# A two-layer diffusion backbone on one core: output projections with a PSUM bank per half, layer 1's last rows, another pool order in the context FFN

## The chip, the core and the metric

The kernel runs on one core of a Trainium2 chip. Its engines work side by side and wait for each other through semaphores: TensorE (PE; PEld is its weight load) multiplies matrices into PSUM, VectorE (DVE), ScalarE (ACT) and GpSimd (POOL) work on elements, and SyncE (SP) issues most DMAs. POOL issues DMAs too. The time of a kernel is the device time of one execution in microseconds (us); the median of several runs counts. A profile is the record of one execution.

## What is computed

Two layers over 1024 latent rows of 1024 numbers (`x`) and 256 context rows (`ctx`). The reference, cut to the flow:

```python
for l in range(DEPTH):                                  # DEPTH = 2
    ctx_out = l < DEPTH - 1                             # the context only in layer 0
    h_lat = modulate(x_lat, m_lat[0], m_lat[1])
    ...
    y_lat, y_ctx = even_mixer(...) or odd_mixer(...)    # attention, then @ w_out
    x_lat = layer_norm(DN_ALPHA * x_lat + m_lat[2] * y_lat, ln_g[l, 0], ln_b[l, 0])
    f_lat = conv_ffn(modulate(x_lat, m_lat[3], m_lat[4]), ffn_w_up[l], ...)
    x_lat = layer_norm(DN_ALPHA * x_lat + m_lat[5] * f_lat, ...)
    if ctx_out:
        ...                                             # the same for x_ctx
return x_lat

def conv_ffn(h, w_up, conv_w, conv_b, w_down):          # 3 taps along the rows
    u = h @ w_up                                        # 1024 -> 2 * 2816
    ...
    a, g = jnp.split(acc, 2, axis=-1)
    return (jax.nn.silu(g) * a) @ w_down
```

All is float32. The kernel keeps that precision with three matmuls for each product: an operand is split into a high part (`h`: a cast on ACT) and a low part (`l`: the rest, a subtraction on DVE or POOL), and `mm3` adds high by high, high by low and low by high. "A weight split" below is one such cast and one such subtraction of 128x512 numbers.

## The kernel before

The stages follow one another: layer 0's projections and attention, its output projection (`l0_out`), the context FFN (`ffn`), the latent FFN of layer 0, then layer 1's projection, attention, output projection (`l1_out`) and FFN. The change touches both output projections and the starts of the two FFNs behind them.

**`out_project`** is the output projection of both layers. It goes over tiles of 128 rows: in layer 0 the two context tiles 8 and 9, then the latent tiles 0 to 7; in layer 1 the latent tiles 0 to 7. For each tile SP loads the old row `x` and the attention's output `yr` in two halves; ACT and POOL split it into `yh` and `yl`. TensorE makes 48 matmuls of 128x512 into the tile `o`: 8 blocks `k` of the contraction by 2 halves `h` of the columns by 3. They run with `k` outside, except in the last tile, where `h` is outside. Behind the last matmul DVE evicts both halves: `hst` (times the gate), a `scalar_tensor_tensor` with the old row, `bn_stats`. `ln` normalises: `mv` on DVE, `rs` on POOL, then the row on DVE (in the last tile half on DVE, half on ACT, with `nm`). `finish` of a tile comes behind the matmuls of the next one: eight transposes (`tr`) on TensorE, eight steps on ACT that modulate them into `hst`, the parts `h2l..` or `h3l..` that the FFN multiplies, sums and differences of blocks (`tt`, called T below) that POOL stores in DRAM, and the store of the row `x`. In the last tile `finish` of the tile before is called between the halves. The hooks are `mid` (in the third tile), `after` (behind the last tile's matmuls) and `last` (at the end).

**End of layer 0.** `after` is `first_up`: it loads and splits the up weights of the first three steps of the context FFN (f = 0, 1, 2; two loads and eight splits each) and makes `u` of two steps (`ctx_up`). `ffn` then goes over 22 steps f: load a down row (`row(f)`, a tile `raw`) and the up weights two steps ahead (`raws[f + 2]`), make `u[f]`, run the convolution of step f - 1 on ACT (`centre`: `a` and `g`) and DVE (`sides`), Silu on ACT, multiply into `gT`, split weights, and multiply step f - 2 down into `d`. The stage's order on each engine is that of the code. Its first DMA is the gate. Where its buffers lie in SBUF follows from the order in which its pools are opened: `acc` (gate, rows), `fraw` (raw weights), `fc` (`a`, `g`), `fg` (`gT`). They take the room that the projection's pools leave, and the first use of a buffer waits for the last use of what lay there.

**End of layer 1.** The FFN behind it multiplies blocks of rows (0 to 511 and 512 to 1023) in seven products for each step, into the PSUM tiles `x`, `y`, `q` and `v`, from `h3lah/h3lal`, `h3lbh/h3lbl` and four operands T0 to T3. `build_B1` makes a tile's share of T0 to T3 for the latent tiles 4 to 7, the last one's straight into the ring of weights, the others' in `tt` (one buffer), stored to `T1` in DRAM and loaded back (`gk`, `go`, `ua`, `ug`) when all are there; ACT and DVE then split them (`T0h`, `T0l`). In `l1_out`, `mid` is `weights` (the up weights of two steps in parts `E[p]`), `after` is `first_x` (the first part of `x` for p = 0 and 1) and `last` is `rest` (more splits). The FFN opens with matmuls that start `y` and `q` (`adds`: dummies of the right shape), a copy of `x` into `y` on ACT, and the second part of `x`, from `h3lbh`; then `v` from T0, `y` from T1, `q` from T2 and T3.

## Time and profile before

| | us |
|---|---|
| median of 3 runs (2916.8 to 2927.06) | 2923.64 |
| the profiled execution | 2927.96 |
| its span | 2926.1 |
| busy: TensorE, DVE, ACT, POOL | 2765.7, 2117.6, 1383.0, 691.5 |
| mean granted clock of TensorE | 0.976 |

The profile's times count from the start of the span, in us. A row of the timeline has its start, its duration, the engine, the line, the operation with what it writes and reads, and in brackets how long the engine had been idle and what ended that. SP's and POOL's DMA rows give the time of the issue, not of the transfer. Matmuls overlap, so their pace is the distance of their starts. In layer 0 the output projection runs from about 754 to 875, in layer 1 from about 2153 to 2250.

### The profile page before, as it was taken

The numbers are of one execution on the slowest core, as the hardware profiler recorded it, in microseconds if no ns is written. First come the engines' busy times: TensorE is split into PE (matmuls) and PEld (weight loads), VectorE is DVE, ScalarE is ACT, GpSimd is POOL, SyncE is SP. The second block draws the span as 40 slices with busy tenths as digits, with TensorE's granted clock in tenths as the row PEclk, the third lists the DMA queues.
The fourth block names the chain that finished last, engine by engine and source line by source line (L and its number), as shares of the span: only waits on it lengthen the run. The fifth ranks groups of instructions, "written<-read, shape, count | busy, mean of one in ns | idle before, by whom it ended". The sixth has DMA issues, their size and how long they took to land.

```text
span 2926.1 us, 45178 instructions
## 1 busy us (share of the span) xinstructions
PE 2765.7 (95%) x16596; PEld 2254.8 (77%) x16596; DVE 2117.6 (72%) x3832; ACT 1383.0 (47%) x2597; POOL 691.5 (24%) x967
## 2 busy tenths in 40 slices
PE   6989999899999999999999987989998899999997
PEld 4877777777788988888888876866677688887886
DVE  4876366667588778888877656557766788888778
ACT  3221255567435655555553342257753545555541
POOL 2611143354451000000001013435544011111002
PEclk8999999999999999999999998989999999999999
DMA  8468711032567653333367526732244455555862
GB/s 261 141 188 275 229 39 41 11 128 94 160 161 241 207 169 107 119 107 114 117 236 272 163 83 195 226 106 64 65 132 146 126 172 164 176 171 201 325 219 93
DMA packets 370502, 456.87 MB, mean 156 GB/s; under 512 B 26137, under 2 KB 265017, under 8 KB 368745
## 3 DMA queue, kind: packets, MB, share of 16 engines
q1 hardware_dynamic: 342808, 369.40, 40.7%
q0 software_dynamic: 24576, 82.89, 8.2%
q8 instruction: 130, 2.13, 0.3%
q10 hardware_dynamic: 2896, 1.70, 0.2%
q14 instruction: 92, 0.75, 0.1%
HBM read 337.98 MB, written 115.93 MB: 155 GB/s over the span
## 4 chain that ended last, share of the span: by engine, by line
PE 68%; issue 10%; DVE 9%; DMA 6%; ACT 5%; POOL 1%; SPq 0%; ACTq 0%; DVEq 0%; POOLq 0%
PE q L1691 8%; PE x L1691 8%; PE y L1691 7%; PE S L762 4%; PE v L1691 4%; PE pv L907 3%; PE T L893 3%; PE dy L2354 3%; PE mm L401 2%; PE d L402 2%; PE d L403 2%; PE d L401 2%; PE mm L402 2%; PE mm L403 2%; PE dx L2354 2%
## 5 line engine op out<-in xcount | busy, mean ns | idle before, releaser
L786 POOL TENSOR_SCALAR P<-P,rin 128x640 f32<-128x640 f32 (+3 forms) x288 | 250.2, 873 | 347.3 <-DVE rin L785 324.0
L1665 DVE TENSOR_TENSOR w<-raw,w 128x512 fp32r<-128x512 f32 x308 | 207.3, 687 | 84.2 <-ACT w L1663 84.1
L112 ACT CAST w<-raw 128x512 fp32r<-128x512 f32 x315 | 183.3, 620 | 171.3 <-PE d L403 60.9
L113 DVE TENSOR_TENSOR w<-raw,w 128x512 fp32r<-128x512 f32 x299 | 194.2, 690 | 70.3 <-ACT w L112 68.2
L762 PE MATMUL S<-k,q 64*128 64x256 f32 (+2 forms) x1824 | 192.4, 338 | 16.9 <-DVE nm L2643 8.1
L783 ACT ACTIVATE P<-P,nm 128x641 f32<-128x641 f32 (+4 forms) x208 | 161.3, 777 | 83.0 <-DVE nm L2643 47.8
L1663 ACT CAST w<-raw 128x512 fp32r<-128x512 f32 x308 | 182.2, 621 | 13.8 <-DVE raw L1670 7.4
L762 PEld LDWEIGHTS S<-k,q 64*128 64x128 f32 x1824 | 136.1, 189 | 52.6 <-issue 17.8
L773 ACT COPY PT<-T 128x512 f32<-128x512 f32 (+1 forms) x250 | 134.0, 565 | 78.9 <-PE T L893 76.7
L907 PE MATMUL pv<-PT,v 128*64 128x128 f32 x2016 | 134.1, 281 | 16.3 <-ACT PT L773 14.1
L893 PE MATMUL T<-ident,P 128*128 128x128 f32 x1008 | 137.2, 283 | 7.9 <-POOL P L786 3.4
L907 PEld LDWEIGHTS pv<-PT,v 128*64 128x64 f32 x2016 | 109.5, 138 | 42.4 <-ACT PT L773 23.0
L401 PE MATMUL d<-w,w 128*128 128x512 f32 x352 | 138.0, 392 | 0.0
L403 PE MATMUL d<-w,w 128*128 128x512 f32 x352 | 137.7, 391 | 0.0
L402 PE MATMUL d<-w,w 128*128 128x512 f32 x352 | 137.6, 391 | 0.0
L785 DVE RECIPROCAL rin<-den 128x1 f32<-128x1 f32 x288 | 46.2, 162 | 121.0 <-ACT P L783 118.1
L893 PEld LDWEIGHTS T<-ident,P 128*128 128x128 f32 x1008 | 111.0, 143 | 28.5 <-issue 14.6
L771 DVE COPY PT<-T 128x512 f32<-128x512 f32 (+1 forms) x166 | 110.4, 666 | 30.7 <-PE T L893 20.6
L1691 PE MATMUL q<-T2h,w 128*128 128x512 f32 x352 | 117.7, 396 | 5.5 <-ACT q L1906 3.9
L1691 PE MATMUL q<-T3h,w 128*128 128x512 f32 x352 | 118.3, 397 | 4.0 <-DVE ug L2309 3.9
L2354 PE MATMUL dy<-w,w 128*128 128x512 f32 x528 | 120.8, 390 | 0.6 <-DVE w L113 0.6
L2643 DVE CUSTOM_DVE_ANT_0 P<-S,msk,snk 128x640 f32<-128x640 f32 (+1 forms) x128 | 103.7, 846 | 16.9 <-PE S L762 13.5
(417 smaller groups left out, 7802.2 us busy)
## 6 DMA issues: line engine op xcount, KB each, us to landing
raw<-in_up_dram SPq DMA_DIRECT2D x132, 512.0 KB
raw<-in_down_dram SPq DMA_DIRECT2D x59, 512.0 KB
raw<-g SPq DMA_DIRECT2D x44, 512.0 KB
raw<-G SPq DMA_DIRECT2D x38, 512.0 KB
araw<-in_ada_w_dram SPq DMA_DIRECT2D x32, 512.0 KB
raw<-in_w_in_dram SPq DMA_DIRECT2D x28, 512.0 KB
g<-cv POOLq DMA_DIRECT2D x22, 512.0 KB, 3.0
G<-go POOLq DMA_DIRECT2D x44, 256.0 KB, 2.7
```

The source lines that it names most:

```text
L112: nc.scalar.copy(hi, s)
L113: (lo_eng or nc.vector).tensor_sub(lo, s, f32(hi))
L401: nc.tensor.matmul(ps, lh, rh, start=first, stop=False)
L402: nc.tensor.matmul(ps, lh, rl, start=False, stop=False)
L403: nc.tensor.matmul(ps, ll, rh, start=False, stop=last)
L762: self.nc.tensor.matmul(outs[a], q[r, x, qs], k[r, y, ks], start=(i == 0), stop=(i == 2))
L786: nc.gpsimd.tensor_scalar(P[:, :n], P[:, :n], rin, 1.0, ALU.mult, ALU.mult)
L893: nc.tensor.transpose(ps[:, s * 128 : (s + 1) * 128], P[a][:, cols[i + x] : cols[i + x] + 128], self.ident,)
L907: nc.tensor.matmul(O[a * HD : (a + 1) * HD], v_of(a, vts[i + x]), pT[:, s * 128 : (s + 1) * 128], start=(i + x == 0), stop=(i + x == m - 1 ...
L1665: nc.vector.tensor_sub(half(i, 1), src[i], f32(half(i, 0)))
L1691: nc.tensor.matmul(ps, w[:, a, s], r[b][:, k], start=first and k + i == 0, stop=k == 3 and i == 2, skip_group_check=True,)
L2354: nc.tensor.matmul(banks[q][t], ga[i][:, a, c], wd[i][:, b], start=q < 2 and f + k == 0, stop=f == HF - 1 and k == 2, skip_group_check=True,)
```

## The change

1. Each half of `o` is a PSUM tile of its own (`o0`, `o1`). In all tiles but the first the half is the outer loop, and the eviction of a half stands behind its own last matmul. In layer 1 these tiles have one buffer each instead of two of the double size; the bank that this leaves holds `y` in the pool of `x`.
2. `first_up` ends with a Silu of one column.
3. `ffn` opens its pools in the order `fc`, `fg`, `fraw`, `acc`.
4. In layer 1, tile 6's T is made in buffers of `yh` and `yl` instead of `tt` and stored in two DMAs. `weights` splits one more part of `E[1]`; `first_x` starts `y` and copies `x` into it; `rest` makes the second part of `x`; the FFN's opening keeps only the dummies of `q`.

```diff
@@ out_project
-            ps = self.t(pp, [128, 2, 512], "o")
+            ps = [self.t(pp, [128, 512], f"o{h}") for h in range(2)]
...
-            if t == order[-1]:
+            if t != order[0]:
                 kh.sort(key=lambda x: x[1])
...
+            g = gate_of(t)
+            s6 = self.t(st, [128, 2, 6], "s6", bufs=3)
             for i, (k, h) in enumerate(kh):
...
                 self.mm3(
-                    ps[:, h], yh[:, k], yl[:, k], ws[k, h][:, 0], ws[k, h][:, 1],
+                    ps[h], yh[:, k], yl[:, k], ws[k, h][:, 0], ws[k, h][:, 1],
                     k == 0, k == KT - 1,
                 )
...
+                if k == KT - 1:
+                    s = slice(h * 512, (h + 1) * 512)
+                    tt = self.t(st, [128, 512], "hst", bufs=3)
+                    nc.vector.tensor_mul(tt, ps[h], g[:, s])
+                    nc.vector.scalar_tensor_tensor(
+                        x[:, s], x[:, s], ALPHA, tt, ALU.mult, ALU.add
+                    )
+                    nc.vector.bn_stats(s6[:, h, :], x[:, s])
@@ first_up
+                warm = self.t(st, [128, 1], "warm")
+                nc.scalar.activation(warm, self.mhalf[:, :1], AF.Silu)
@@ ffn
-            ap = es.enter_context(self.pool("acc"))
-            raw = es.enter_context(self.pool("fraw", bufs=4))
             cvp = es.enter_context(self.pool("fc", bufs=2))
             gp = es.enter_context(self.pool("fg", bufs=3))
+            raw = es.enter_context(self.pool("fraw", bufs=4))
+            ap = es.enter_context(self.pool("acc"))
@@ build_B1
+        elif t == NLAT - 2:
+            m = [
+                self.t(st, [128, KT, 128], x, bufs=2).rearrange("p (m k) j -> p m k j", m=2)
+                for x in ("yh", "yl")
+            ]
+            tt = [m[i // 2][:, i % 2] for i in range(4)]
...
-        if t < NLAT - 1:
+        if t == NLAT - 2:
+            for i in range(2):
+                nc.gpsimd.dma_start(
+                    dT[2 * i : 2 * i + 2, :, t - 4].rearrange("m p k j -> p m k j"), m[i]
+                )
+        elif t < NLAT - 2:
             nc.gpsimd.dma_start(dT[:, :, t - 4].rearrange("m p k j -> p m k j"), m)
@@ layer 1's FFN, opening
                     for p in pre if m == 1 else []:
-                        X, Y, Q = YQ[p] = (early["x", p],) + tuple(
-                            self.t(pu, [128, 512], f"{x}{p}") for x in "yq"
-                        )
-                        adds(Y, Q)
-                        nc.scalar.copy(Y, X)
-                        self.product(early[p][0][2], b21, X, False)
+                        Q = self.t(pu, [128, 512], f"q{p}")
+                        YQ[p] = early["x", p], early["y", p], Q
+                        adds(Q)
@@ l1_out
-            pp = es.enter_context(self.pool("op1", bufs=2, space=PSUM))
+            pp = es.enter_context(self.pool("op1", bufs=1, space=PSUM))
...
-                for p, i in ((0, 0), (1, 0), (0, 2), (0, 1)):
+                for p, i in ((0, 0), (1, 0), (0, 2), (1, 2), (0, 1)):
                     self.some_parts(E[p][1], [i])
 
             def first_x():
                 for p in range(2):
-                    E["x", p] = self.t(px, [128, 512], f"x{p}")
-                    self.product(E[p][0][0], h2l[:2], E["x", p], True)
+                    X, Y = (self.t(px, [128, 512], f"{x}{p}") for x in "xy")
+                    E["x", p], E["y", p] = X, Y
+                    ah = h2l[0]
+                    nc.tensor.matmul(Y, ah[:, 0, :128], ah[:, 0], start=True, stop=True)
+                    self.product(E[p][0][0], h2l[:2], X, True)
+                    nc.scalar.copy(Y, X)
 
             def rest():
+                for p in range(2):
+                    self.product(E[p][0][2], [v[:, :, 0] for v in h2l[2:]], E["x", p], False)
                 self.some_parts(E[0][1], [4, 3, 5, 6])
-                self.some_parts(E[1][1], [2])
```

What this moves on the engines, at three places. First SP at the end of layer 0, with what each DMA waits for: the last up load of `first_up`, then the context FFN's gate, its first down row and the up weights of step 3. Before:

```order
L1644 DMA raw_10012<-in_up_dram 128x8x128 [waits DVE_49]
L159 DMA gate_10182<-ada_89 128x1024 [waits PE_49]
L1440 DMA raw_10188<-in_down_dram 128x1024 [waits DMAHW2_49,PE_49]
L1644 DMA raw_10190<-in_up_dram 128x8x128 [waits DVE_49]
L1644 DMA raw_10192<-in_up_dram 128x8x128 [waits DMAHW4_49,DVE_49]
```

Now:

```order
L1657 DMA raw_10022<-in_up_dram 128x8x128 [waits DVE_49]
L159 DMA gate_10194<-ada_89 128x1024 [waits DMASW7_49,DVE_49,DMAHW7_49,PE_49,Activation_49]
L1442 DMA raw_10200<-in_down_dram 128x1024 [waits DMAHW2_49]
L1657 DMA raw_10202<-in_up_dram 128x8x128
L1657 DMA raw_10204<-in_up_dram 128x8x128 [waits DMAHW4_49]
```

The order is the same. The gate waited for TensorE alone and now waits for a DMA of POOL's queue (the store of tile 7's row), DVE, SP's own load of that row, TensorE and ACT, since the gate's buffer lies where that row lay; the loads behind it lost most waits of their own.

ACT at the same place, from the half row of tile 7 (`x`) on: `hst` are tile 7's transposes, `a` and `g` step 0 of the context FFN, `w` its down weights. Before:

```order
L372 ACTIVATE x_9869<-x_9869,nm_9943,rs_9940 128x512
L1556 ACTIVATE hst_10130<-tr_10125,m1ab_572_3199 128x128 x4
L1556 ACTIVATE hst_10143<-tr_10138,m1ab_572_3199 128x128 x4
L1444 ACTIVATE a_10196<-u_10026,cc_369_1685,cc_367_1681 128x256
L1444 ACTIVATE g_10198<-u_10026,cc_369_1685,cc_367_1681 128x256
L1488 ACT_TABLE_LOAD
L1488 ACTIVATE g_10198<-g_10198 128x256
L1495 CAST gT_10206<-a_10196 128x256
L112 CAST w_10209<-raw_10188 128x512
```

Now:

```order
L372 ACTIVATE x_9879<-x_9879,nm_9953,rs_9950 128x512
L1446 ACTIVATE a_10208<-u_10036,cc_369_1685,cc_367_1681 128x256
L1446 ACTIVATE g_10210<-u_10036,cc_369_1685,cc_367_1681 128x256
L1490 ACTIVATE g_10210<-g_10210 128x256
L1497 CAST gT_10218<-a_10208 128x256
L1558 ACTIVATE hst_10142<-tr_10137,m1ab_572_3199 128x128 x4
L1558 ACTIVATE hst_10155<-tr_10150,m1ab_572_3199 128x128 x4
L112 CAST w_10221<-raw_10200 128x512
```

Step 0's convolution, Silu and `gT` moved ahead of tile 7's transposes, and the table load in front of Silu is gone from here (it stands with the new Silu, far ahead).

DVE at the end of layer 1, from tile 7's first eviction (`hst` from `o`) to its statistics; `tt`, `yh` and `yl` are tile 6's T. Before:

```order
L1310 TENSOR_TENSOR hst_23503<-o_23410,gate_22667 128x512
L1311 SCALAR_TENSOR_TENSOR x_23411<-x_23411,hst_23503 128x512
L1622 TENSOR_TENSOR tt_23469<-hst_23452,h3lah_22647 128x512
L1625 TENSOR_TENSOR tt_23469<-hst_23462,hst_23452 128x512
L1623 TENSOR_TENSOR tt_23469<-tt_23469,h3lal_22648 128x512
L1314 BN_STATS s_4542_23502<-x_23411 128x6
L1624 TENSOR_TENSOR tt_23469<-hst_23462,tt_23469 128x512
L1310 TENSOR_TENSOR hst_23507<-o_23410,gate_22667 128x512
L1626 TENSOR_TENSOR tt_23469<-h3lbh_22649,tt_23469 128x512
L1311 SCALAR_TENSOR_TENSOR x_23411<-x_23411,hst_23507 128x512
L1627 TENSOR_TENSOR tt_23469<-tt_23469,h3lbl_22650 128x512
L1314 BN_STATS s_4542_23502<-x_23411 128x6
```

Now:

```order
L1310 TENSOR_TENSOR hst_23471<-o_4550_23432,gate_22679 128x512
L1311 SCALAR_TENSOR_TENSOR x_23434<-x_23434,hst_23471 128x512
L1314 BN_STATS s_4557_23446<-x_23434 128x6
L1630 TENSOR_TENSOR yh_23497<-hst_23480,h3lah_22659 128x512
L1631 TENSOR_TENSOR yh_23497<-yh_23497,h3lal_22660 128x512
L1607 CAST h3lbh_22661<-hst_23490 128x4x128
L1632 TENSOR_TENSOR yh_23497<-hst_23490,yh_23497 128x512
L1633 TENSOR_TENSOR yl_23498<-hst_23490,hst_23480 128x512
L1634 TENSOR_TENSOR yl_23498<-h3lbh_22661,yh_23497 128x512
L1635 TENSOR_TENSOR yl_23498<-yl_23498,h3lbl_22662 128x512
L1310 TENSOR_TENSOR hst_23532<-o_4551_23433,gate_22679 128x512
L1311 SCALAR_TENSOR_TENSOR x_23434<-x_23434,hst_23532 128x512
```

The second half's `hst` stood in the midst of tile 6's T and now stands behind all of it; the first half's three steps stand together in front.

17 lines of the change are left out of this document (4 added, 13 removed).

## The prediction

> **What bounds the kernel now.** I read the page first: its busy table and the chain that ended last.
>
> ```profile
> PE 2765.7 (95%) x16596; PEld 2254.8 (77%) x16596; DVE 2117.6 (72%) x3832; ACT 1383.0 (47%) x2597; POOL 691.5 (24%) x967
> PE 68%; issue 10%; DVE 9%; DMA 6%; ACT 5%; POOL 1%; SPq 0%; ACTq 0%; DVEq 0%; POOLq 0%
> ```
>
> TensorE is busy for 95% of the span and carries most of the chain. The change removes no matmul of weight, so it can win only where TensorE waits. I listed TensorE's waits in the two stretches that the diff touches: the end of layer 0's output projection (870 to 906 us), then the end of layer 1's (2230 to 2320 us). Columns: instruction, what ended the wait, us in total, times, longest.
>
> ```profile
> PE d L401 <- ACT w L112: 4.5, 1, 4.5
> PE tr L1550 <- ACT x L372: 1.2, 1, 1.2
> ...
> PE tr L1588 <- issue: 4.2, 1, 4.2
> PE q L1691 <- DVE ug L2309: 3.0, 1, 3.0
> PE x L1691 <- ACT w L1663: 2.9, 1, 2.9
> PE tr L1588 <- DVE x L373: 2.1, 1, 2.1
> PE x L1691 <- ACT y L2247: 1.8, 1, 1.8
> ...
> PE x L1691 <- DVE w L1665: 0.8, 1, 0.8
> ```
>
> That is 5.7 us in the first stretch and 11.8 in the second, without the 3.0 behind `ug`, which lies later, in the products' own chain. Next, the table by stretch: layer 1's steady tiles, then the clock in two places (PE, PEld, DVE, ACT, POOL busy; granted clock, DMA share, GB/s).
>
> ```profile
> 2176.00:2235.50 59.50, 59.50 (x287) 49.74 (x286) 39.59 (x58) 20.23 (x50) 35.11 (x34) 1.00 0.38 132
> 900.00:905.00 5.00, 5.00 (x12) 3.59 (x13) 4.78 (x10) 3.68 (x8) 0.00 (x0) 0.50 0.00 1
> 2243.50:2249.00 5.50, 5.44 (x28) 4.69 (x29) 3.02 (x5) 2.90 (x8) 2.66 (x3) 1.00 0.47 179
> ```
>
> TensorE has no gap in the steady tiles. Behind the 4.5 us wait the clock fell to 0.50; behind the 2.1 us wait it stayed at 1.00. So a long wait costs twice.
>
> **End of layer 0.** Start, duration, engine, line, out<-in; in brackets the idle time before and what ended it.
>
> ```profile
> 879.84 1.14 ACT L112 CAST w<-raw 128x512 fp32r<-128x512 f32 x2 [7.40 <-DMA raw<-in_up_dram]
> 887.25 0.81 ACT L372 ACTIVATE x<-x,nm,rs 128x512 f32<-128x512 f32 x1 [2.66 <-DVE nm L371]
> 893.42 0.56 ACT L1444 ACTIVATE a<-u,cc,cc 128x256 f32<-128x256 f32 x1 [1.24 <-DMA x<-x]
> 896.64 1.28 ACT L1488 ACT_TABLE_LOAD   x1 [2.20 <-DVE g L1451]
> 899.16 1.14 ACT L112 CAST w<-raw 128x512 fp32r<-128x512 f32 x2
> 873.38 0.37 SPq L1644 DMA_DIRECT2D raw<-in_up_dram  x1
> 873.79 0.71 SPq L159 DMA_DIRECT2D gate<-ada  x1
> 889.04 0.57 POOL L1367 DMA_DIRECT2D x<-x  x1 [0.82 <-issue]
> 881.11 1.28 DVE L1310 TENSOR_TENSOR hst<-o,gate 128x512 f32<-128x512 f32 x2
> 888.61 1.06 PE L1550 MATMUL tr<-ident,x 128*128 128x128 f32 x8 [1.17 <-ACT x L372]
> 899.82 0.80 PE L401 MATMUL d<-w,gT 128*128 128x512 f32 x1 [4.45 <-ACT w L112]
> 905.26 0.28 PE L401 MATMUL u<-h2ch,w 128*128 128x256 f32 x1
> ```
>
> Now: the last tile's eviction (881.11) stands on DVE behind a weight split whose load left at 873.38 and landed at 879.84, 6.46 us later. The normalised row follows at 887.25 and its store at 889.04, and `a<-u` waits until that store has landed (893.42), because its buffer lies where the row lay. The table load, Silu and casts follow, then `d`.
>
> After: tile 6's first half and tile 7's are evicted early, so the late load leaves sooner and only one half is left behind it. Of the six eviction steps (some 0.6 us each by the 1.28 for two) I count on three: the row at 885, 2 us earlier. TensorE then transposes when it is free, at 888.61 - 1.17 = 887.4: the 1.2 us go. `a<-u` no longer waits for the store, and the table load is gone from there. From `a<-u` to `d` took 6.4 with the load, 5.1 without; started at 886, that chain is ready at 891, before the third `u` ends at 899.82 - 4.45 = 895.4, less those 1.2: 894.2.
>
> What comes late next is `d`'s weight. In the new order the gate's load waits for the last tile's store, and `row(0)` and the loads of up f=3 stand behind it on SP's queue. They left from 873.79 on; now not before the row at 886 plus the store's 4.4 (889.04 to 893.42) and an issue each: near 891 for the gate, 891.8 for `row(0)`. That takes between 4.4 (like the store) and 6.46 (like the load): landed at 896.2 to 898.3. From its cast to `d` is 0.66 (899.16 to 899.82): `d` at 896.9 to 898.9. Its 12 matmuls took 5.44 at half clock (899.82 to 905.26) and take 2.7 at full clock; `u` behind them also needs f=3 split. I put `u` at 901 to 903 in place of 905.26: **gain 3.5**, with bounds 6.5 (loads in 4.4, full clock) and -11 (first rival).
>
> The Trainium skill ("TensorE: Matmul & The Clock Gate", What's actually happening) says that the clock halves after an idle window of about 3.4 us and recovers after a busy window as long. The 0.50 behind 4.45 us and the 1.00 behind 2.05 agree. By that rule a gap under 3 us before `d` would often leave it at full clock, and the sum would be 2.7 larger, an estimate.
>
> **End of layer 1.**
>
> ```profile
> 2235.02 1.04 PE L1588 MATMUL tr<-ident,x 128*128 128x128 f32 x8
> 2243.56 1.06 PE L1588 MATMUL tr<-ident,x 128*128 128x128 f32 x8 [2.05 <-DVE x L373]
> 2249.95 0.39 PE L1691 MATMUL x<-h3lah,w 128*128 128x512 f32 x1
> 2259.75 1.57 PE L1588 MATMUL tr<-ident,x 128*128 128x128 f32 x8 [4.20 <-issue]
> 2277.30 0.39 PE L1691 MATMUL v<-T0h,w 128*128 128x512 f32 x1
> 2280.04 0.39 PE L1691 MATMUL y<-T1h,w 128*128 128x512 f32 x1
> 2283.87 0.50 PE L1691 MATMUL q<-T2h,w 128*128 128x512 f32 x1 [0.95 <-ACT q L2291]
> 2240.62 0.92 DVE L1622 TENSOR_TENSOR tt<-hst,h3lah 128x512 f32<-128x512 f32 x1 [0.90 <-DMA T<-tt]
> 2250.15 0.69 DVE L1310 TENSOR_TENSOR hst<-o,gate 128x512 f32<-128x512 f32 x1 [2.57 <-PE o L403]
> 2257.60 0.21 DVE L357 BATCH_NORM_AGGREGATE mv<-s 128x2 f32<-128x12 f32 x1
> 2262.10 0.69 DVE L1622 TENSOR_TENSOR w<-hst,h3lah 128x512 f32<-128x512 f32 x1 [2.45 <-ACT hst L1594]
> 2270.23 1.22 DVE L1721 TENSOR_TENSOR T0l<-gk,T0h 128x1024 fp32r<-128x1024 f32 x1 [0.88 <-ACT T0h L1720]
> 2271.37 1.89 DVE L1665 TENSOR_TENSOR w<-raw,w 128x512 fp32r<-128x512 f32 x3
> 2273.78 0.69 DVE L1721 TENSOR_TENSOR T0l<-w,T0h 128x512 fp32r<-128x512 f32 x1
> ```
>
> The pace at full clock: `v`'s 12 matmuls take 2.74 (2277.30 to 2280.04), so 24 take 5.5; eight transposes take what is left of 2243.56 to 2249.95, 0.9.
>
> *Tile 6's transposes.* Half of its eviction is done before its matmuls end, so three DVE steps less stand ahead of its row, and the store that `tt` waited for (0.90) leaves earlier. I estimate the row 2.5 us earlier; the wait is 2.05. Transposes at 2241.5: gain 2.05, all of it.
>
> *Tile 7's transposes.* Its first half could only be evicted at 2250.15, because both halves were one PSUM tile. Then 12 DVE steps of 0.62 (2250.15 to 2257.60) evict both halves and build tile 6's T; row and transposes follow 2.15 later. After: the first half is free at 2241.5. I estimate that DVE has done tile 5's leftovers, that half, and tile 6's T (seven steps) by 2250. The second half ends at 2241.5 + 0.9 + 5.5 = 2247.9, is evicted by 2252.2, and the transposes go at 2254.3. TensorE's `x` products (24 matmuls, two dummies: 5.9) end at 2253.8: a wait of 0.5 in place of 4.20.
>
> *`x<-h3lbh` and `v`.* The second part of `x` needs nothing of tile 7, and its copies and weights are made earlier now. It follows the transposes at once, 24 matmuls and two dummies, to 2261.1; the waits of 1.8, 2.9 and 0.8 go. What is late next is T0's low half. DVE's run for it took from 2262.10 to 2274.47; without the three weight subtractions in it (1.89, now elsewhere) and its wait on ACT (0.88, a cast behind a copy that moves), 9.6. It starts 2.2 behind the transposes and lasts from 2256.5 to 2266.1. So `v` starts near 2266.1, not 2277.30: 11.2 earlier, but behind a new wait of 5 us, longer than the 4.45 that halved the clock. At half clock its 12 matmuls take 5.4, and `q` follows 3.8 behind `v`'s end as now (2280.04 to 2283.87, a row of ACT copies and casts): 2275.4 in place of 2283.87. **Gain 8.5**, with bounds 11 (full clock) and 5 (DVE's run lasts 12.4 as now, less the waits that go all the same). Nothing behind is tied to fixed times: the later waits follow TensorE's own products.
>
> **Steady tiles, half-major with a bank per half: nothing.** DVE has 59.50 - 39.59 = 19.9 us free between 2176 and 2235.5, so the earlier evictions find room. The earlier split for `E[1]` (a cast and a subtraction, 1.2 us) hides under those full matmuls; without that cover it costs the 1.2. Layer 1's `o0` and `o1` have one buffer each, so a half waits for its eviction in the tile before; the other half's 5.5 us cover that. The warm-up Silu stands on ACT among the casts of the projection's first weights, ahead of its matmuls; its table load is 1.28. For all this I take 0, between a loss of 1.3 and a gain of 1.
>
> **Sum.** 3.5 + 8.5 = 12 us. The profiled execution took 2927.96 (span 2926.1); against it that is 2916.0. It lies 4.3 above the median of the three runs, 2923.64, so I predict 2911.6.
>
> **Rivals.**
>
> - *Layer 0's loads starve.* Eight loads of 0.52 MB and the last stores, 5 MB together, now leave within a few us. At the rate of the row below that is 20 us. If they advance side by side, `row(0)` lands near 910 and `u` starts 11 us late; with layer 1's gain the time is then 2926. A middle case loses 5: 2920. For it: these loads start 17 us later than now. Against: a load among others landed in 6.46. Chance 0.13.
>
> ```profile
> 880.00:895.00 15.00, 13.84 (x118) 1.00 0.89 254
> ```
>
> The Trainium skill ("DMA: Bandwidth & Descriptors", Issuing engines are not separate DMA queues) says that DMAs of all issuers run on the same 16 engines and interleave; if so here, POOL's stores slow the loads too.
>
> - *Layer 1's wait only moves.* DVE, not TensorE, sets the end there. If its run to T0l still takes 12.4, layer 1 gains 5, and with half of layer 0's gain the sum is 7: 2917. For it: my chain on DVE has no slack. Against: the weight subtractions have left it. Chance 0.17.
> - *Slower: layer 1's single banks.* If DVE comes to a half's eviction more than 5.5 us after its matmuls, TensorE stops in that tile. The sign turns where the three tiles with T work lose over 4 each; at 7 each the time is 2933. For it: the row and four subtractions of an older tile now stand ahead of such an eviction. Against: 19.9 us free on DVE. Chance 0.05.
> - *No effect*: other waits take the place of those that go: 2923. Chance 0.05.
>
> **How the numbers follow.** The forecast has 0.60; alone it lies between 2906 and 2915. A measurement tells 0.3%, 8.8 us, from no change, so faster means under 2914.8: 0.64 with a little of the second rival; within 0.3% 0.29; slower 0.07. The range goes from the bounds 6.5 and 11 together, less three us of scatter (the three runs lie 10 apart), 2903, up to the middle of the first rival with as much scatter, 2922.
>
> **What would show it.** Right: no table load before the first Silu of the context FFN; the gate's load near 891 and `d` near 898; transposes of tiles 6 and 7 with waits under 1; one wait of about 5 before `v`, ended by DVE's `T0l`, the clock near half behind it. Wrong: `d` no earlier than now; a wait of `o` on `hst` in layer 1; `v` less than 6 us earlier against the transposes at 2235.02.

## The result, and the profile after

| | before | after |
|---|---|---|
| median, us (9 runs each, same chip) | 2923.47 | 2911.78 |
| lowest and highest | 2916.8, 2927.48 | 2901.51, 2915.36 |
| the profiled execution, its span | 2927.96, 2926.1 | 2915.36, 2913.5 |

The ratio is 0.9951, with a 95% interval from 0.9942 to 0.9960: the change makes the kernel 0.49% faster, clear of 0.3%. The forecast was 2911.6.

To see where the time went I cut both profiled executions at the same instructions of TensorE and subtracted the starts. These five pieces make up the whole difference:

| from | to | before | after | difference |
|---|---|---|---|---|
| start | `tr` of latent tile 6, layer 0 | 875.03 | 878.39 | +3.4 |
| that | the second block of `d` | 35.93 | 30.61 | **-5.3** |
| that | `tr` of tile 5, layer 1 | 1324.06 | 1321.43 | -2.6 |
| that | the first `q` from T2h | 48.85 | 42.15 | **-6.7** |
| that | end | 642.23 | 640.92 | -1.3 |

The first and the last piece hold none of the code that gains, and over the fourteen profiled executions of this study they scatter by more than they differ here: `tr` of tile 6 came between 870.1 and 885.2. Layer 0's steady tiles lie in the first and took as long as before, 120.5 and 120.4 from the first `o` to `tr` of tile 6. The third holds layer 1's steady tiles, which took as long as before: from layer 1's first `o` to `tr` of tile 5 81.83 before and 81.93 after. The gain is at the two ends that the prediction named.

TensorE's waits at these two ends, after (instruction, what ended the wait, us in total, times, longest), first at layer 0's end (870 to 906 us), then at layer 1's (2140 to 2320 us):

```profile
PE d L401 <- ACT w L112: 2.0, 1, 2.0
PE u L403 <- DVE w L113: 0.2, 1, 0.2
...
PE v L1704 <- DVE T0l L1734: 3.0, 1, 3.0
PE q L1704 <- DVE ug L2320: 3.0, 1, 3.0
PE tr L1590 <- issue: 2.9, 1, 2.9
PE q L1704 <- ACT q L2302: 1.7, 2, 1.0
PE tr L1590 <- DVE x L373: 0.7, 1, 0.7
...
PE o L401 <- DVE hst L1310: 0.2, 1, 0.2
```

In layer 0 one wait of 2.0 is left of 4.5 and 1.2. In layer 1 the waits of `x` for `w` and `y` (2.9, 1.8, 0.8) are gone, `tr` keeps 2.9 and 0.7, and a new wait of 3.0 stands before `v`. The table by stretch (PE, PEld, DVE, ACT, POOL busy; granted clock, DMA share, GB/s) has the steady tiles, the stretch behind the 2.0 wait, two behind the 2.9 wait, and one behind the 3.0 wait:

```profile
2171.50:2231.00 59.50, 59.50 (x287) 49.57 (x286) 52.49 (x62) 19.96 (x50) 33.78 (x35) 1.00 0.37 130
...
900.00:905.00 5.00, 4.65 (x26) 3.99 (x27) 4.78 (x10) 3.31 (x7) 0.00 (x0) 1.00 1.10 359
...
2253.00:2257.70 4.70, 4.70 (x18) 3.88 (x19) 2.45 (x5) 4.70 (x13) 1.16 (x2) 0.64 0.78 219
2257.70:2261.00 3.30, 3.30 (x16) 2.71 (x15) 3.30 (x4) 3.30 (x6) 1.11 (x1) 1.00 0.42 168
2264.70:2267.50 2.80, 2.73 (x7) 2.16 (x8) 2.80 (x5) 0.00 (x0) 0.00 (x0) 0.50 0.81 277
```

Layer 0's clock stays at 1.00, where it was 0.50 before. Layer 1's falls twice. The steady tiles still keep TensorE busy without a gap, but DVE is now busy for 52.49 of 59.50 us there instead of 39.59.

The timeline of layer 0's end, after (start, duration, engine, line, out<-in, idle time before and what ended it):

```profile
886.89 0.81 ACT L372 ACTIVATE x<-x,nm,rs 128x512 f32<-128x512 f32 x1 [1.90 <-DVE nm L371]
887.61 0.55 ACT L1446 ACTIVATE a<-u,cc,cc 128x256 f32<-128x256 f32 x1
891.08 0.42 ACT L1490 ACTIVATE g<-g 128x256 f32<-128x256 f32 x1 [2.47 <-DVE g L1453]
898.72 1.14 ACT L112 CAST w<-raw 128x512 fp32r<-128x512 f32 x2 [3.51 <-DMA raw<-in_down_dram]
892.84 0.33 SPq L159 DMA_DIRECT2D gate<-ada  x1
893.22 0.46 SPq L1442 DMA_DIRECT2D raw<-in_down_dram  x1
888.70 0.57 POOL L1367 DMA_DIRECT2D x<-x  x1 [0.82 <-ACT g L1446]
890.65 1.04 PE L1552 MATMUL tr<-ident,x 128*128 128x128 f32 x8
899.39 0.51 PE L401 MATMUL d<-w,gT 128*128 128x512 f32 x1 [2.00 <-ACT w L112]
902.74 0.28 PE L401 MATMUL u<-h2ch,w 128*128 128x256 f32 x1
```

`a<-u` follows the row without a wait, no table load stands before Silu, and `tr` waits for nothing. What is late is the weight: the gate's load leaves at 892.84, 4.1 behind the issue of the row's store, the first down row right behind it, and that has landed 5.5 us later, at 898.72.

The same for layer 1's end:

```profile
2230.43 1.04 PE L1590 MATMUL tr<-ident,x 128*128 128x128 f32 x8
2252.95 1.07 PE L1590 MATMUL tr<-ident,x 128*128 128x128 f32 x8 [2.91 <-issue]
2264.76 0.80 PE L1704 MATMUL v<-T0l,w 128*128 128x512 f32 x1 [3.01 <-DVE T0l L1734]
2272.58 0.50 PE L1704 MATMUL q<-T2h,w 128*128 128x512 f32 x1 [0.99 <-ACT q L2302]
2234.50 0.69 DVE L1630 TENSOR_TENSOR tt<-hst,h3lah 128x512 f32<-128x512 f32 x1 [1.66 <-DMA T<-tt]
2238.32 1.92 DVE L1633 TENSOR_TENSOR tt<-hst,hst 128x512 f32<-128x512 f32 x1
2241.48 0.68 DVE L1310 TENSOR_TENSOR hst<-o,gate 128x512 f32<-128x512 f32 x1
2245.80 1.80 DVE L1633 TENSOR_TENSOR yl<-hst,hst 128x512 f32<-128x512 f32 x1
2248.84 0.68 DVE L1310 TENSOR_TENSOR hst<-o,gate 128x512 f32<-128x512 f32 x1
2255.22 0.69 DVE L1630 TENSOR_TENSOR w<-hst,h3lah 128x512 f32<-128x512 f32 x1 [2.37 <-ACT hst L1596]
2264.03 0.68 DVE L1734 TENSOR_TENSOR T0l<-w,T0h 128x512 fp32r<-128x512 f32 x1
2238.38 1.30 POOL L1608 TENSOR_TENSOR h3lbl<-hst,h3lbh 128x512 fp32r<-128x512 f32 x1
2245.37 1.68 POOL L1608 TENSOR_TENSOR h3lbl<-hst,h3lbh 128x512 fp32r<-128x512 f32 x1 [2.70 <-DVE h3lbh L1607]
```

From here on DVE sets the pace: 2230.43 to the last row's `tr` at 2252.95 is DVE's work on tile 5's T, both halves of tile 7 and tile 6's T, and 2255.22 to 2264.71 is its run to T0l.

### The profile page after: what moved, and what is told of

The parts are those of the page before. It is cut to its first block, busy times and chain, and to the rows that moved or that the text cites. A ratio compares the mean times of both kernels' runs of the same rounds, so it can differ in the third digit from the quotient of the medians.

```text
span 2913.5 us, 45188 instructions
## 1 busy us (share of the span) xinstructions
PE 2761.8 (95%) x16596; PEld 2251.1 (77%) x16596; DVE 2139.0 (73%) x3832; ACT 1382.7 (47%) x2598; POOL 691.7 (24%) x968
## 4 chain that ended last, share of the span: by engine, by line
PE 67%; DVE 10%; issue 10%; DMA 7%; ACT 4%; POOL 1%; SPq 0%; ACTq 0%; DVEq 0%; POOLq 0%
PE q L1704 8%; PE x L1704 7%; PE y L1704 7%; PE S L762 5%; PE v L1704 4%; PE pv L907 3%; PE T L893 3%; PE dy L2365 3%; PE mm L401 3%; PE mm L402 2%; PE mm L403 2%; PE d L401 2%; PE d L402 2%; PE d L403 2%; PE dx L2365 2%
## 5 line engine op out<-in xcount | busy, mean ns | idle before, releaser
L771 DVE COPY PT<-T 128x512 f32<-128x512 f32 (+1 forms) x166 | 110.4, 666 | 30.6 <-PE T L893 20.5
L1704 PE MATMUL v<-T0h,w 128*128 128x512 f32 x352 | 116.4, 392 | 0.0
```

The lines of the kernel that those rows point to most:

```text
L1704: nc.tensor.matmul(ps, w[:, a, s], r[b][:, k], start=first and k + i == 0, stop=k == 3 and i == 2, skip_group_check=True,)
```

## The experiments

A trial that shifts 1 or 2 us can't be told by the time alone, whose intervals are about 0.12% (3.5 us) to each side. So each is read twice: by its ratio to the kernel before, in the same series, and by two stretches of its trace. **L0** is from `tr` of tile 6 to the second block of `d` in layer 0, **L1** from `tr` of tile 5 to the first `q` from T2h in layer 1, both as in the table above. Runs with the same layer 1 code give L1 48.6 to 50.4 for the code before and 41.3 to 43.3 for the code after: differences below 2 us between single runs tell little there. The series ran on different chips, where the kernel before took 2925.2 to 2928.22, so medians of different series are compared by their ratios.

| run | median | ratio, 95% interval | L0 | L1 |
|---|---|---|---|---|
| before | 2923.47 | 1 | 35.9 | 48.9 |
| after | 2911.78 | 0.9951 (0.9942 to 0.9960) | 30.6 | 42.2 |
| pool order alone | 2926.91 | 0.9996 (0.9985 to 1.0006) | 35.7 | 48.6 |
| pool order, early Silu | 2925.84 | 0.9993 (0.9984 to 1.0002) | 35.9 | 50.4 |
| after, old pool order | 2915.01 | 0.9959 (0.9945 to 0.9973) | 33.3 | 41.3 |
| after, layer 1's rows undone | 2923.82 | 0.9981 (0.9969 to 0.9994) | 30.8 | 51.3 |
| gate later | 2911.91 | 0.9950 (0.9938 to 0.9963) | 29.3 | 43.3 |
| T0 before the splits | 2918.26 | 0.9968 (0.9957 to 0.9980) | 30.8 | 44.8 |
| tile 6's T in `tt` | 2913.89 | 0.9955 (0.9942 to 0.9967) | 30.8 | 45.0 |
| dummies before `v` | 2910.35 | 0.9947 (0.9933 to 0.9960) | 30.8 | 41.4 |
| layer 1 with a whole tile of two banks | 2938.89 | 1.0047 (1.0033 to 1.0061) | 31.7 | 53.2 |
| no early Silu | 2911.21 | 0.9955 (0.9942 to 0.9969) | 30.8 | 42.4 |
| gate later, T0 first, dummies | 2914.45 | 0.9957 (0.9944 to 0.9971) | 29.2 | 43.3 |
| gate later, dummies | 2910.57 | 0.9944 (0.9931 to 0.9958) | 29.3 | 41.3 |

**Layer 0: which part gains?** First the pool order alone, on the kernel before:

```diff
-            ap = es.enter_context(self.pool("acc"))
-            raw = es.enter_context(self.pool("fraw", bufs=4))
             cvp = es.enter_context(self.pool("fc", bufs=2))
             gp = es.enter_context(self.pool("fg", bufs=3))
+            raw = es.enter_context(self.pool("fraw", bufs=4))
+            ap = es.enter_context(self.pool("acc"))
```

> The kernel before with the new pool order of the context FFN alone. Theory A (the late weight is the bound): the last row comes no earlier than before, the gate's load now waits for its store (landed 893.4 in the trace of before), so row(0) leaves near 894 and d starts near 900, behind a wait near 5 us and at half clock: within 2 us of the kernel before. Rival B (the wait of a<-u for the store was the bound, and the pool order carries the gain of layer 0): d 3 to 6 us earlier against tile 6's transposes, and a time 3 to 6 us below before.

The same with the early Silu:

```diff
+                warm = self.t(st, [128, 1], "warm")
+                nc.scalar.activation(warm, self.mhalf[:, :1], AF.Silu)
```

> Pool order and the early Silu of one column, the rest as before. Theory A: as the run with the pool order alone, within 1 us, since d's weight and not gT is late. Rival C (the table load of 1.28 us stood on the chain to d): d 1.3 us earlier than with the pool order alone.

And the reverse, the changed kernel with the pools in the old order:

```diff
+            ap = es.enter_context(self.pool("acc"))
+            raw = es.enter_context(self.pool("fraw", bufs=4))
             cvp = es.enter_context(self.pool("fc", bufs=2))
             gp = es.enter_context(self.pool("fg", bufs=3))
-            raw = es.enter_context(self.pool("fraw", bufs=4))
-            ap = es.enter_context(self.pool("acc"))
```

> The changed kernel with the old pool order. Theory A: a<-u waits for the last row's store again (landed near 893 in the changed kernel's trace), but the weights are loaded early; without the table load d comes some 5 us behind that, 898 to 899, 0 to 1.5 us earlier than in the changed kernel counted from tile 6's transposes; time within 2 us of the changed kernel. Rival B (pool order carries layer 0's gain): d 3 to 6 us later, time near 2917.

TensorE's wait for the first `d`, in the waits of the kernel with the pool order alone, then of the changed kernel with the old order, and behind it ScalarE's row that begins the chain to `d` in that kernel:

```profile
PE d L401 <- ACT w L112: 4.6, 1, 4.6
```

```profile
PE d L401 <- ACT w L112: 3.7, 1, 3.7
```

```profile
889.63 0.57 ACT L1446 ACTIVATE a<-u,cc,cc 128x256 f32<-128x256 f32 x1 [1.93 <-DMA x<-x]
```

With the new order and the early Silu it is 4.8. The new order alone gains nothing. It takes `a<-u` off the store, but puts the gate's load behind it, and while the row is as late as before, the weight that follows comes just as late. The halves with the early Silu but without the new order gain 2.6 in L0: the row is earlier, but `a<-u` waits for its store, 1.93. Theory A for the old order had `d` up to 1.5 earlier than in the changed kernel, counted from `tr` of tile 6; it came 1.7 later. Together they gain 5.3, more than 0.3 and 2.6: with the row early the weight behind the gate is ready 1.7 sooner than the chain behind `a<-u` would be, and behind the shorter wait (2.0 for 3.7) the clock holds. `d`'s first block to the next `u` is 3.35 after, 4.88 with the old order, 5.37 with the new order alone.

The changed kernel without the early Silu:

```diff
-                warm = self.t(st, [128, 1], "warm")
-                nc.scalar.activation(warm, self.mhalf[:, :1], AF.Silu)
```

> The changed kernel without the one-column Silu that ScalarE runs early in layer 0's end. Theory A (it saves a table load of 1.3 us which is beside the wait for the second-layer weights): the table load is back in front of the first Silu of the FFN, d is not later (8.7 to 9.0 after the transpose of tile 7, as in the changed kernel), and the time stays within 1 us. Rival L (ScalarE is the chain there, since the Silu is followed by gT, the last tile's eviction and the cast of w): d comes 1.3 us later and the time is 1.3 us more, with the clock fallen behind the longer wait up to 3.

`d` came 8.92 behind `tr` of tile 7, against 8.74 to 9.19 in the runs that have the early Silu and the same layer 0, and the ratios are 0.9955 and 0.9951. It is worth nothing that can be seen here: the table load is back in front of Silu but ends before the weight arrives.

If the weight's load behind the gate is the bound, moving the gate must move `d`:

```diff
-            self.bcast(gate, gate_row)
             x = [self.t(ap, [128, D], f"x{t}") for t in range(nt)]
...
                 if f == 4:
+                    self.bcast(gate, gate_row)
```

> The changed kernel with one call moved: layer 0's FFN broadcasts its gate row in the last pass, before the first second-layer block, and no longer ahead of the weight loads. SP's loads then stand behind no wait for the last latent tile's store. Theory A (layer 0's end is bound by the row's store, then the gate's load, then the first row of second-layer weights behind it in SP's queue): the 2.0 wait of TensorE for the cast of w goes, d begins when u's last block ends, 2.0 us earlier after the transpose of tile 7 (8.74 to about 6.7), the casts of w run before ScalarE's Silu, and the time is about 2 us below the changed kernel's, near 2909 to 2910. Rival D (the first weights are bound by landing, about 5.5 us after they are issued, or by buffers that come free): the wait stays between 1 and 2 us and the time stays within 1 us. Rival E: the gate, loaded later, comes too late for its own consumer, VectorE's add behind d, which adds a wait of some us there.

It did: `d` begins without a wait, 6.58 behind `tr` of tile 7 instead of 8.74. But its second matmul then waits, 1.46, now for DVE:

```profile
896.11 0.50 PE L402 MATMUL d<-w,gT 128*128 128x512 f32 x1 [1.46 <-DVE w L113]
```

DVE's half of that split stands behind the subtractions for the last tile's T. Of 2.2 that `d` gained, 1.3 arrive at its second block (L0 29.3), and the time can't tell this from the changed kernel. Theory A had the bound right and the sum too large.

**Layer 1: what carries the gain?** The whole of part 4 undone (tile 6's T, the copies, the second part of `x`, the split), with the halves kept:

```diff
-        elif t == NLAT - 2:
-            m = [
-                self.t(st, [128, KT, 128], x, bufs=2).rearrange("p (m k) j -> p m k j", m=2)
...
-                for p, i in ((0, 0), (1, 0), (0, 2), (1, 2), (0, 1)):
+                for p, i in ((0, 0), (1, 0), (0, 2), (0, 1)):
...
-                    X, Y = (self.t(px, [128, 512], f"{x}{p}") for x in "xy")
...
+                    E["x", p] = self.t(px, [128, 512], f"x{p}")
...
+                self.some_parts(E[1][1], [2])
```

> The changed kernel without its part 4: tile 6's T in the single tt, the early split of E[1], y's start and copy and the second part of x as before; halves, banks and pool order stay. Theory: the waits before the second part of x come back (1.8, 2.9 and 0.8 in the trace of before), and tile 6's T waits for a store again, so layer 1 keeps 2 to 4 of its 6.7 us: 3 to 5 us slower than the changed kernel, 2915 to 2917. Rival (the half banks carry all of layer 1's gain, DVE's run to T0l is the bound in any case): within 1.5 us of the changed kernel.

Waits of TensorE in its timeline:

```profile
2255.04 1.94 PE L1590 MATMUL tr<-ident,x 128*128 128x128 f32 x8 [5.19 <-issue]
2259.67 0.80 PE L1693 MATMUL x<-h3lbh,w 128*128 128x512 f32 x1 [1.84 <-ACT y L2249]
2268.82 0.50 PE L1693 MATMUL x<-h3lbh,w 128*128 128x512 f32 x1 [2.85 <-ACT w L1665]
```

I had expected the halves to keep some of layer 1's gain. They keep none: L1 is 51.3, 9.1 longer than after and 2.4 longer than before. All of layer 1's gain, and a little more, is part 4's. So is the time: 0.9981 against 0.9951 is 0.30%, 8.8 us.

One piece of it, tile 6's T back in the single buffer:

```diff
-        elif t == NLAT - 2:
-            m = [
...
-        if t == NLAT - 2:
...
-        elif t < NLAT - 2:
+        if t < NLAT - 1:
             nc.gpsimd.dma_start(dT[:, :, t - 4].rearrange("m p k j -> p m k j"), m)
```

> The changed kernel with the transposed halves of latent tile 6 in the single buffer tt and stored to DRAM in one transfer, as for the tiles before it, where the change put them into pairs of buffers of their own. Theory A (the buffer is what the chain at layer 1's end gains by): VectorE waits for the store of tile 5's T before it writes tile 6's, which lands near 2246.5 and so some 3 us after the write began in the changed kernel; the transpose of tile 7 comes 2 to 3 us later, its wait grows from 2.9 to 5 to 6 us, and the time is 2 to 3 us above the changed kernel's, near 2914 to 2915. Rival H (the store is done by then, the buffers were worth nothing and part 4's gain is all in the earlier splits and the T kept on chip for tile 7): the wait stays at 2.9 and the time within 1 us.

```profile
2239.91 0.69 DVE L1624 TENSOR_TENSOR tt<-hst,h3lah 128x512 f32<-128x512 f32 x1 [2.58 <-DMA T<-tt]
```

DVE waits 2.58 for tile 5's store, `tr` of tile 7 comes 17.14 behind that of tile 6 instead of 15.34, and L1 is 45.0, 1.7 to 3.7 above the runs of the changed code. That fits theory A's 2 to 3 us, which the ratio (0.9955) can't tell, though the wait of `tr` did not grow to 5: one of the two products `x<-h3lbh`, which need nothing of tile 7, now stands ahead of it, and the wait shows up before `v` (3.0 for T0h, then 4.4). Of part 4's 9.1 some 6 are left. The waits of `x` in the rows above (5.3 with one of 0.6) would make up most of them; the copies, the split and the moved product were not tried one by one.

What would the same copies cost without a bank per half? The rival of the prediction that ends slower lived there. Layer 1's `o` as one tile of two banks, in one buffer:

```diff
-            ps = [self.t(pp, [128, 512], f"o{h}") for h in range(2)]
+            if mid is not None:
+                o = self.t(pp, [128, 2, 512], "o")
+                ps = [o[:, h] for h in range(2)]
+            else:
+                ps = [self.t(pp, [128, 512], f"o{h}") for h in range(2)]
```

> The changed kernel with layer 1's output projection in one single-buffered tile of two banks in place of two single-buffered halves; everything else as changed, and the copies moved up stay, so this is what they would cost without a bank per half. Theory A (the two halves are what lets layer 1 give up its second pair of banks): each tile's first o waits until both halves of the tile before are evicted; the last eviction begins as the last product ends and takes 0.68, with the last tile's product of the scale row behind it, less the transposes that stand between tiles (1 us), so 1 to 2.5 us and a fallen clock for each of seven tiles, 10 to 25 us in all, 2922 to 2937. Rival K: the transposes and the first weights of a tile cover the eviction, the waits stay below 0.3 each and the time stays within 2 us of the changed kernel's.

```profile
PE o L401 <- DVE hst L1314: 12.2, 9, 2.8
PE tr L1594 <- DVE x L373: 6.6, 6, 1.6
```

The waits of `o` on the eviction come, 12.2 us in nine waits, and with those of `tr` and the T chain behind them the kernel is 0.47% slower than before and 0.96% (28 us) slower than the changed kernel, a little more than theory A's 10 to 25. Layer 1's halves gain nothing by themselves, but they pay for part 4: with them one buffer is enough, which frees the bank for `y`.

**What is left at layer 1's end.** Does the 3.0 wait before `v` cost twice? Idle matmuls fill it, into a bank that is overwritten before it is read:

```diff
-                        adds(Q)
+                        adds(*[Q] * 8)
```

> The changed kernel with eight passes of idle matmuls in place of one in front of the pass that begins with v <- T0l; they write a bank that nothing reads, so the outputs are the same. Theory A (the wait of 3.0 us costs twice: once as a wait, and again because the granted clock falls behind it and the next products run at half speed for about 2.7 us): TensorE is busy through the wait, v begins at the same time or up to 0.3 later, the products behind it run at full speed, and 1 to 1.5 us go from the stretch between v <- T0l and q <- T2h. Rival I: the clock follows something longer than this one wait, the products stay at half speed, and nothing goes. Rival J: the dummies outlast the wait and cost 0.5 us or more.

TensorE's clock in the product behind them, in the table by stretch (0.50 for the same product in the table above):

```profile
2258.60:2261.10 2.50, 2.03 (x9) 1.32 (x8) 2.50 (x5) 0.48 (x2) 0.00 (x0) 1.00 0.89 296
```

The clock holds, but from `v` to `q` it took 7.3 instead of 7.8, where theory A had 1 to 1.5 less, and L1, 41.4, lies within the 41.3 to 43.3 of the changed code. That scatter lies behind `v`. In all four runs of that code `v<-T0l` begins 34.3 behind `tr` of tile 5. From there to `q` it took 7.0 with the old pool order, where the clock stayed at 1.00 behind the same wait of 3.00 without any dummies, and 7.8, 8.1 and 9.0 in the other three, where it fell (behind 3.0, 4.6 and 3.0). It held in both runs with eight dummies (7.3 and 7.2). So by these runs a fallen clock here costs 0.8 to 1.9 us; that the dummies prevent it is likely, not shown.

Can T0l come earlier? The weight splits that stand before it, moved behind T0 and T1 on both engines:

```diff
                         make_T(0)
+                        if pre:
+                            early["late"](4)
                         make_T(1)
+                        if pre:
+                            early["late"](3, 5, 6)
...
-                self.some_parts(E[0][1], [4, 3, 5, 6])
+                E["late"] = lambda *i: self.some_parts(E[0][1], i)
```

> The changed kernel with the splits of the last pass's weights (four parts of E[0], two engines) moved from in front of the making of T0 to behind it. Theory A (layer 1's end: VectorE and ScalarE are the chain from x of the last row to T0h and T0l, and the splits in front of it lengthen it): the wait of v for T0l falls from 3.0 to about 1.2 us, TensorE's clock does not fall behind it, and 2.3 to 3.3 us go, near 2909. Rival F: the splits were beside other waits, T0l comes no earlier, and the wait stays at 3.0. Rival G: the splits, now later, make the next reader of E[0] wait as long as was gained (y <- T1 or q), so that the sum from tr of tile 5 to q of T2h stays at 42 us.

```profile
2258.26 0.50 PE L1704 MATMUL v<-T0l,w 128*128 128x512 f32 x1 [1.29 <-DVE T0l L1734]
2270.41 0.79 PE L1704 MATMUL q<-T2h,w 128*128 128x512 f32 x1 [4.64 <-ACT q L2306]
```

The wait of `v` fell to 1.29 as theory A said, and `q` then waited 4.64: rival G, and worse, since L1 is 44.8 where that rival left it at 42. ScalarE's casts of these splits wait for VectorE's sums of raw weights, and they now stood ahead of the copy of `v` and of `q` in ScalarE's queue. A second try moved only VectorE's half of two parts, and the other two parts behind T2. Beside layer 0's later gate and four passes of idle matmuls its edit is:

```diff
-                self.some_parts(E[0][1], [4, 3, 5, 6])
+                call = E[0][1]
+                call("s", 4)
+                call("h", 4)
+                call("h", 3)
...
                         make_T(0)
+                        if pre:
+                            early[0][1]("l", 4)
                         make_T(1)
+                        if pre:
+                            early[0][1]("l", 3)
+                            early[0][1]("s", 5)
...
                         make_T(2)
+                        if pre:
+                            early[0][1]("h", 5)
+                            early[0][1]("l", 5)
+                            early[0][1]("s", 6)
+                            early[0][1]("h", 6)
+                            early[0][1]("l", 6)
```

> A version meant to beat both: the changed kernel with layer 0's FFN gate loaded in the pass before its first second-layer block, as in the first of the second series; at layer 1's end VectorE makes T0l before its half of the weight splits of parts 4 and 3, the splits of parts 5 and 6 go behind T2 on both engines, and four passes of idle matmuls in place of one fill the rest of TensorE's wait. Theory A (T0's chain on VectorE and the clock behind the wait are what is left there, and the fault of the earlier trial was that casts waiting for VectorE stood ahead of the copy of v in ScalarE's queue): T0l comes 1.8 us earlier, no wait of v above 0.5, q of T2h not later, so 1.5 to 3 us at layer 1's end and 1.4 us at layer 0's: 2907 to 2910. Rival M: q <- T2 waits for the split of part 5 as long as was gained, and only layer 0's 1.4 us are left.

```profile
2268.85 1.14 ACT L1676 CAST w<-raw 128x512 fp32r<-128x512 f32 x2 [2.14 <-DVE raw L1683]
2269.90 0.58 ACT L2313 COPY q<-y 128x512 f32<-128x512 f32 x1
```

`v` waited for nothing, but a cast that waits for VectorE still stood before `q<-y`, held for 2.14, and `q` waited 4.2. Only layer 0's gain was left, as rival M had it: the splits took back at `q` what `v` had gained. Last, only the two trials whose stretch had become shorter, together:

```diff
-            self.bcast(gate, gate_row)
...
+                    self.bcast(gate, gate_row)
...
-                        adds(Q)
+                        adds(*[Q] * 8)
```

> The two trials whose stretch became shorter, and nothing else: the changed kernel with layer 0's FFN gate loaded in the pass before its first second-layer block, and eight passes of idle matmuls in place of one at layer 1's end, into a bank that nothing reads. Theory A (both act in their own place, and nothing behind takes them back): from the transpose of tile 7 to the second d of layer 0 17.0 in place of 18.35; from the transpose of tile 7 to q of T2h at layer 1's end 18.9 in place of 19.6 to 20.8; 2 to 3 us in all, near 2909, a ratio to before of 0.9940 to 0.9947. Rival N: what is gained in front of the next stage is taken back by it, or is lost in the scatter of the stages between, which was some us between runs of the same code: the ratio is that of the changed kernel, 0.9951, within 0.0006.

L0 is 29.3 and L1 41.3, both as in the single trials; from `tr` of tile 7 it took 17.0 to the second `d` and 18.8 to `q`, as expected. The ratio is 0.9944, the lowest of all, with an interval that holds 0.9951. It is faster than the kernel before; that it beats the changed kernel can't be told by the time. Layer 0's part is seen in the stretches: 29.2 to 29.3 in all three runs with the later gate, 30.6 to 31.7 in the seven that differ there only by the early gate or the early Silu. Layer 1's part is not: the old pool order had 41.3 and 18.8 without dummies.

## Why the prediction was right, and where it was not

The sum was 3.5 at layer 0's end and 8.5 at layer 1's, 12 together. The two stretches show 5.3 and 6.7, 12 together. The total is right because two errors cancel, which is luck.

**Layer 0: the term was too small.** The mechanism was the one named: row earlier, `a<-u` free of the store, the down row behind the gate's load as the last one. Counted from `tr` of tile 6, the row came 3.7 earlier (12.22 to 8.50), not 2, and the gate left 14.45 behind it, not 16. The landing, 5.5, lay between the 4.4 and the 6.46 of the text. So `d` gained 3.8 where 0.9 to 2.9 stood. The rest is the clock. The wait is 2.0, and the clock stayed at 1.00 behind it, so `u` gained 5.9, of which 0.6 went again in `u` itself before the second `d`; I had chosen a value between the half and the full clock. The sentence that drew on the Trainium skill ("TensorE: Matmul & The Clock Gate", What's actually happening) would have added 2.7 to the sum, 6.2 for this end; the trace sided with it. Other runs are less clear: before this `d` the clock stayed at 1.00 behind waits of 2.0 to 2.3 in six of them and fell to 0.50 behind 2.45 in the whole-tile trial.

**Layer 1: the step that failed is DVE's chain to tile 7's transposes.** The text gave them a wait of 0.5, 19.3 behind `tr` of tile 5; they came at 22.5 with a wait of 2.9. It had DVE done with tile 5's leftovers, the first half and tile 6's T 15.0 behind `tr` of tile 5 (2250 against 2235.02). The second half's eviction, which follows that work, began at 2248.84, 18.4 behind it. Three rows hold more than these 3.4: DVE waits 1.66 for the store of tile 4's T before it writes tile 5's, and two subtractions take 1.92 and 1.80 where the text counted 0.62. They run beside POOL's `h3lbl` (2238.38 and 2245.37). The profile before had shown both lengths of this subtraction (count, then the shortest, median and longest in ns, and the first and last start):

```profile
L1625 DVE TENSOR_TENSOR tt<-hst,hst x3: 678/683/1793, 2229.6 to 2252.1; 128x512 f32<-128x512 f32 x3
```

The longest, at 2229.57, is the one that ran beside POOL's `h3lbl`. I had taken one mean for all steps. Tile 6's transposes missed in the same way, by less: they kept a wait of 0.69 and gained 1.4, not 2.05. The sum of the old waits was short too: it left out 1.6 of `q` on ScalarE's copies, which are still there (1.7).

The Trainium skill ("SBUF — State Buffer", Who interferes with whom) says that a VectorE instruction with two SBUF inputs contends with a GpSimd instruction that reads SBUF, and that the one behind is blocked, not slowed in part. The rows agree: beside POOL the subtraction of two SBUF tiles takes 1.80, while `hst<-o,gate`, one of whose inputs is in PSUM, keeps to 0.67 to 0.69 in all sixteen steps of layer 1's tiles, three of which ran beside POOL's `yl` (2159.71, 2208.34 and 2218.93).

From there on the working held. DVE's run to T0l was put at 9.6, beginning 2.2 behind the transposes; it took 9.5 and began 2.3 behind. `v`'s wait was 3.0 rather than 5, because the clock fell behind the wait of `tr` and `x` took longer. DVE sets this end whatever the clock: in the run without the early Silu the clock stayed up behind `tr`'s 2.90, `v` waited 4.55, and T0l was ready 11.8 behind `tr` of tile 7, as in the changed kernel. From `v` to `q` it took 7.8 rather than 9.2, the clock being back up within 2.8 us; in the other runs of this code that took 7.0 to 9.0, so this part is partly the luck of the run. So 3.2 lost and 1.4 won: 6.7 instead of 8.5.

**What cost nothing** did cost nothing: the steady tiles (81.83 and 81.93) and the early Silu. But the cover shrank. Of DVE's 19.9 us free in 59.5, 7.0 are left.

**The rivals.** *Layer 0's loads starve* did not come: the first load landed in 5.5 with the DMA engines at 297 to 359 GB/s between 895 and 905, and `u` waited 0.2. *Layer 1's wait only moves* has the right sign, too large: a wait did move to `v`, but 6.7 of 8.5 stayed gained. *Slower: single banks* is a real mechanism, as the whole-tile trial shows, but with a bank per half the only trace of it is one wait of 0.2 on `hst`. *No effect* is excluded by the ratio's interval.

**What stays open.** Why the stages of unchanged code before, between and behind differ by several us between runs was not tried. What decides whether the clock falls behind a wait of 2.4 to 3 us is open too: its length alone does not (last section).

## What to carry to other kernels

When a wait at the end of a stage goes, write down the new order of every queue that the moved work shares, and ask for each instruction that waits on another engine who stands behind it: the gate's load held the weights in SP's queue, and casts in ScalarE's queue took back what two trials had gained. A change that gains nothing alone may be what lets another gain: the pool order needed the early row, and the copies moved up needed the bank per half. Take an engine's step times from rows in which its neighbours are as busy as they will be, not from a mean.

## What the runs showed of the hardware

VectorE pays for running beside GpSimd far more than the forecast allowed. In the steady tiles of layer 1 (ten steps each, in the windows of the two tables by stretch) the eviction's `scalar_tensor_tensor` has a mean of 1.29 before and 1.81 after, since the earlier evictions meet POOL's subtractions. That is 5.5 of the 12.9 us that DVE is busier there; the row's normalisation, 0.81 undisturbed and 1.8 beside POOL, is another 2.9. Two of the ten took six times the undisturbed 0.69; this one lasts until POOL's rows beside it have ended (timeline of the changed kernel; DVE, then POOL):

```profile
2194.76 4.30 DVE L1311 SCALAR_TENSOR_TENSOR x<-x,hst 128x512 f32<-128x512 f32 x1
2200.42 0.69 DVE L1311 SCALAR_TENSOR_TENSOR x<-x,hst 128x512 f32<-128x512 f32 x1
```

```profile
2194.72 1.30 POOL L1608 TENSOR_TENSOR h3lbl<-hst,h3lbh 128x512 fp32r<-128x512 f32 x1
2195.98 2.53 POOL L1291 TENSOR_TENSOR yl<-yr,yh 128x512 fp32r<-128x512 f32 x2
```

TensorE's clock does not follow the length of a wait alone. Behind waits of 2.9 to 3.0 it went both ways: in the changed kernel it fell behind `v`'s 3.01, but stayed at 1.00 behind the 2.97 before `q<-T3h` at 2296.45, and with the old pool order it stayed at 1.00 behind `v`'s 3.00. Behind 2.45, in the whole-tile trial before layer 0's `d`, it fell. The stretches right behind these three waits (changed kernel, old pool order, whole-tile trial):

```profile
2296.40:2299.30 2.90, 2.85 (x12) 2.35 (x13) 2.90 (x5) 0.00 (x0) 0.28 (x1) 1.00 0.24 90
2262.50:2265.20 2.70, 2.64 (x11) 2.18 (x12) 2.70 (x5) 0.00 (x0) 0.00 (x0) 1.00 0.87 291
892.40:895.40 3.00, 3.00 (x6) 2.10 (x7) 2.78 (x6) 2.41 (x5) 0.00 (x0) 0.50 1.16 340
```

In the changed kernel it was back after 2.8 to 4.7 us of work. So in these runs a wait of 2.4 to 3 us may cost once or twice, and a single run of such a place can't tell what an edit did to the clock.
